# Residual by channel and projections with stationary weights in a two-layer decoder trunk on one core

## The chip, the core and the metric

One core of a Trainium2 chip runs the whole program. The metric is the device time of one execution in microseconds (us). The engines are TensorE (PE; the loads of its stationary operand are listed as PEld), VectorE (DVE), ScalarE (ACT), GpSimd (POOL) and SyncE (SP, which issues nearly all transfers). L258 is line 258 of the kernel.

## What is computed

256 tokens of width 1024 go through two layers, each with a feed-forward block before and after its mixer; four feed-forward blocks in all (l0a, l0b, l1a, l1b). Inner width is 2816.

```
def _rmsnorm(x, w):
    y = xf * lax.rsqrt(jnp.mean(xf * xf, axis=-1, keepdims=True) + NORM_EPS)
    return (y * w.astype(jnp.float32)).astype(x.dtype)
def _swiglu(h, w_in, w_out):
    gate, up = jnp.split(h @ w_in, 2, axis=-1)
    return (jax.nn.silu(gate) * up) @ w_out
for l in range(DEPTH):
    x = x + 0.5 * _swiglu(_rmsnorm(x, ffn_norm1[l]), ffn1_w_in[l], ffn1_w_out[l])
    h = _rmsnorm(x, mix_norm[l])
    if l % 2 == 0:
        x = x + _hybrid_ab_mixer(h, ...)
    else:
        x = x + _pool_mixer(h, pool_w[i], pool_scale[i])
    x = x + 0.5 * _swiglu(_rmsnorm(x, ffn_norm2[l]), ffn2_w_in[l], ffn2_w_out[l])
return _rmsnorm(x, final_norm)
```

The first mixer joins four gated DeltaNet heads (their inputs pass a short causal convolution) and four spatial-gating groups; the second averages over windows of 2 to 16 tokens.

## The kernel before, in words

**Products in three parts.** Every projection is made to nearly full fp32 accuracy from operands split into a high and a low part: hi is the value cast to fp32r (L213 or L216, ScalarE), lo is the value less hi (L214 or L217, VectorE). A product is then hi x hi + hi x lo + lo x hi, three matmuls that add up in one PSUM bank (`products`, L252 to L258). Transposes, norms and the DeltaNet algebra are plain fp32; an fp32 matmul leaves two records in the trace.

**Weights.** `load_unit` (L178) fetches one unit, mostly 1 MB, into one of four raw buffers and splits it into one of three pairs of hi and lo, 512 columns an instruction. The gain of the RMSNorm, one number per input channel, is multiplied in there (L216, L217 with a scale from `prm`).

**Residual by token.** `x` lies with tokens on the partitions. Before each block, `next_input` (L350) transposes it with TensorE (L249, 16 blocks of 128x128), splits the result into `xth` and `xtl` (channels on the partitions), and `rstd` (L235) makes the norm's factor r of each token, which scales the projections' results later.

**Feed-forward block** (`ffn`, L280). For five chunks of 512 inner columns and one of 256, gate and up are projected for each half t of 128 tokens: the token block is stationary, 512 weight columns move. ScalarE makes silu(r x gate) (L304), VectorE r x up x silu (L312). The hidden values now have tokens on the partitions, so `hidden` (L287) transposes them (L292, 44 blocks a feed-forward) and splits them into `hh` and `hl`. `out_proj` (L320) multiplies them with the output weights, hidden block stationary, 512 columns moving (L325), and VectorE adds half of it to `x` (L345). The last two units are held, so that token half 0 ends early and is prepared under the products of half 1.

**Mixer** (L459). Its projections of ba, z, sv and su work as above; q, k and v pass a convolution along the tokens and are made with the weights stationary and all 256 tokens moving (`conv`, L565, products at L577 to L579), scaled by r along the free axis (`rb`, L561, L562). Its out projection (L805) uses `out_proj`. The pool stage (`pooled`, L410) multiplies a band matrix (L425, L427) and then the pool weights.

The instruction order on each engine is fixed when the program is built: a scheduler places each instruction by its own estimates, so neighbouring steps interleave, but each engine then works through its list in order.

Of the kernel before, what the change touches and what calls it, by code (L numbers as in the profile page):

```python
# [26 lines left out]
WIDE = 130 * LINE  # L27
NEG = -1e30
# [3 lines left out]
FFN_CHUNKS = [(c * 512, 512) for c in range(5)] + [(2560, 256)]  # L32

MIX_CHUNKS = (("ba", 260), ("sv", 512), ("k", 512), ("v", 512), ("q", 512), ("z", 260), ("su", 512))

# [14 lines left out]
def weight_units():  # L50
# [3 lines left out]
    def ffn(name):  # L54
        for c, (_, w) in enumerate(FFN_CHUNKS):
            for part in ("g", "u"):
                halves = 1 if w == 256 else 2
                for h in range(halves):
                    units.append((name, "in", c, part, h, (KD // halves) * w))
        for u in range(NF // 2):  # L60
            units.append((name, "out", u, "", 0, 2 * D))

    ffn("l0a")
    for n, w in MIX_CHUNKS:
        halves = 2 if w == 512 else 1
        for h in range(halves):
            units.append(("mix", "in", n, "", h, KD // halves * w))
    for u in range(4):
        units.append(("mix", "out", u, "", 0, 2 * D))
    ffn("l0b")  # L70
    ffn("l1a")
    units.append(("pool", "w", 0, "", 0, 8 * 256))
# [8 lines left out]
def pack_weights(a):  # L81
# [4 lines left out]
    for name, kind, c, part, h, n in weight_units():  # L86
        if name in ffns:
            base, l = ffns[name]
            if kind == "in":
                c0, w = FFN_CHUNKS[c]  # L90
                c0 += DFF if part == "u" else 0
                rows = n // w * P
                src = a[base + "_w_in"][l][h * rows:(h + 1) * rows, c0:c0 + w]
            else:
                src = a[base + "_w_out"][l][c * 2 * P:(c + 1) * 2 * P]
        elif name == "mix" and kind == "in":
            rows = n // len(cols[c]) * P
            src = a["ab_w_in"][0][h * rows:(h + 1) * rows][:, cols[c]]
        elif name == "mix":
            ks = OUT_ORDER[2 * c:2 * c + 2]  # L100
            src = np.concatenate([a["ab_w_out"][0][k * P:(k + 1) * P] for k in ks])
        else:
            src = a["pool_w"][0].reshape(D, 256)
        k = src.shape[0] // P
        blocks.append(np.ascontiguousarray(src.reshape(k, P, -1).transpose(1, 0, 2)).reshape(-1))
    return np.concatenate(blocks)
# [49 lines left out]
def trunk(ctx: ExitStack, tc: tile.TileContext, x_in, xt_in, wts, prm_in, ident_in, mixc_in, band_in,  # L156
# [13 lines left out]

# [3 lines left out]
    units = weight_units()  # L174
    offsets = np.concatenate([[0], np.cumsum([u[-1] * P for u in units])])
    state = {"u": 0}

    def load_unit(k, col=None, prescale=None):  # L178
# [658 lines left out]
```

## Time and profile before

| | us |
|---|---|
| median of 3 runs (lowest, highest) | 932.19 (931.95, 934.86) |
| the profiled execution | 931.89 |
| its span, first to last instruction | 930.1 |
| PE busy in the span | 916.9 |
| DVE busy | 562.2 |
| ACT busy | 504.1 |

The mean granted TensorE clock was 0.995 of full speed. An engine's busy time is the union of its instructions' times; neighbouring matmuls overlap in the pipeline, so their mean durations don't add up to it, and the distance between starts tells what one costs in a row of many.

### The profile page before, as it was taken

How to read it: one execution, taken by the hardware profiler on the slowest of the kernel's cores; microseconds unless marked ns; L12 is line 12 of the kernel's file. 1: busy time of each engine (PE TensorE's matmuls, PEld its weight loads, DVE VectorE, ACT ScalarE, POOL GpSimd, SP SyncE). 2: the span in 40 equal slices, each digit the busy share in tenths (PEclk: the TensorE clock that was granted, in tenths of full speed). 3: DMA queues.
4: the chain of work that ended last, by engine and by line, in shares of the span. 5: the costliest groups of instructions: out<-in, count | busy, mean ns of one | idle time of the engine just before them, and what ended most of it. 6: DMA issues, size and time to landing. Idle time of an engine off the chain costs nothing.

```text
span 930.1 us, 12029 instructions
## 1 busy us (share of the span) xinstructions
PE 916.9 (99%) x4614; PEld 763.8 (82%) x4614; DVE 562.2 (60%) x987; ACT 504.1 (54%) x930; POOL 29.9 (3%) x44
## 2 busy tenths in 40 slices
PE   8999999999999999999999999999999999999997
PEld 6788888889998788888888888888888888889885
DVE  4765564468997665555644565556556565556444
ACT  6755553387747565555533565556335455556332
POOL 0000000000321000000000000000000000000000
PEclk9999999999999999999999999999999899999999
DMA  8865555534225246555455555555553365554521
GB/s 326 317 226 181 181 181 182 187 137 176 91 92 181 87 142 224 181 181 181 175 188 181 211 198 181 181 181 181 181 184 134 113 228 182 183 181 177 187 85 45
DMA packets 24521, 163.10 MB, mean 175 GB/s; under 512 B 2832, under 2 KB 2960, under 8 KB 5648
## 3 DMA queue, kind: packets, MB, share of 16 engines
q1 hardware_dynamic: 24176, 161.81, 48.9%
q8 instruction: 36, 0.59, 0.3%
q10 hardware_dynamic: 288, 0.52, 0.2%
q14 instruction: 21, 0.17, 0.1%
HBM read 161.28 MB, written 1.05 MB: 175 GB/s over the span
## 4 chain that ended last, share of the span: by engine, by line
PE 90%; DVE 4%; DMA 2%; ACT 2%; issue 1%; POOL 0%; SPq 0%; POOLq 0%; ACTq 0%
PE acc L325 26%; PE mm L258 18%; PE mm L255 18%; PE mm L256 18%; PE acc L292 2%; PE mm L325 2%; DMA x<-in_x 1%; DVE y L586 1%; PE mm L579 1%; PE acc L249 1%; DVE lo L217 1%; PE mm L577 1%; PE mm L578 1%; DMA raw<-in_wts 1%; PE acc L425 1%
## 5 line engine op out<-in xcount | busy, mean ns | idle before, releaser
L216 ACT ACTIVATE hi<-raw,prm 128x512 fp32r<-128x512 f32 (+2 forms) x448 | 268.9, 673 | 169.2 <-PE mm L258 133.7
L217 DVE SCALAR_TENSOR_TENSOR lo<-raw,prm,hi 128x512 fp32r<-128x512 f32 (+2 forms) x448 | 287.5, 699 | 120.9 <-ACT hi L216 120.7
L255 PE MATMUL mm<-hi,xth 128*128 128x512 f32 (+2 forms) x832 | 305.4, 376 | 1.5 <-ACT xth L213 1.5
L256 PE MATMUL mm<-lo,xth 128*128 128x512 f32 (+2 forms) x832 | 303.3, 373 | 0.1
L258 PE MATMUL mm<-hi,xtl 128*128 128x512 f32 (+2 forms) x832 | 207.4, 372 | 0.1
L214 DVE TENSOR_TENSOR lo<-raw,hi 128x512 fp32r<-128x512 f32 x192 | 121.3, 686 | 111.1 <-ACT hi L213 111.1
L255 PEld LDWEIGHTS mm<-hi,xth 128*128 128x128 f32 x832 | 156.5, 188 | 31.2 <-ACT xth L213 2.3
L256 PEld LDWEIGHTS mm<-lo,xth 128*128 128x128 f32 x832 | 156.6, 188 | 28.9 <-DVE lo L217 0.5
L213 ACT CAST hi<-raw 128x512 fp32r<-128x512 f32 x192 | 106.5, 619 | 131.1 <-PE acc L325 108.6
L258 PEld LDWEIGHTS mm<-hi,xtl 128*128 128x128 f32 x832 | 146.1, 188 | 29.7 <-DVE xtl L214 0.9
L325 PE MATMUL acc<-hi,hh 128*128 128x512 f32 x352 | 140.1, 398 | 0.0
L325 PE MATMUL acc<-hi,hl 128*128 128x512 f32 x352 | 138.7, 394 | 0.0
L325 PE MATMUL acc<-lo,hh 128*128 128x512 f32 x352 | 138.4, 393 | 0.0
L325 PEld LDWEIGHTS acc<-hi,hh 128*128 128x128 f32 x352 | 66.1, 188 | 15.9 <-DVE hl L214 1.2
L325 PEld LDWEIGHTS acc<-hi,hl 128*128 128x128 f32 x352 | 66.0, 188 | 15.7
L325 PEld LDWEIGHTS acc<-lo,hh 128*128 128x128 f32 x352 | 66.2, 188 | 14.4
L304 ACT ACTIVATE sg<-mm,r 128x512 f32<-128x512 f32 (+1 forms) x48 | 31.3, 653 | 54.8 <-PE mm L258 51.6
L214 DVE TENSOR_TENSOR hl<-acc,hh 128x512 fp32r<-128x512 f32 (+1 forms) x48 | 29.1, 640 | 49.5 <-ACT hh L213 49.5
L312 DVE SCALAR_TENSOR_TENSOR hid<-mm,r,sg 128x512 f32<-128x512 f32 (+1 forms) x48 | 33.7, 703 | 30.7 <-PE mm L258 30.7
L233 POOL TENSOR_TENSOR r<-ms,mhalf 128x1 f32<-128x1 f32 x14 | 8.6, 613 | 790.9 <-DVE ms L242 790.9
L239 ACT ACTIVATE junk<-x 128x512 bf16<-128x512 f32 x28 | 17.6, 629 | 24.1 <-DVE x L345 20.2
L579 PE MATMUL mm<-xth,lo 128*128 128x256 f32 x96 | 27.4, 286 | 0.0
(177 smaller groups left out, 601.7 us busy)
## 6 DMA issues: line engine op xcount, KB each, us to landing
raw<-in_wts SPq DMA_DIRECT2D x145, 1024.0 KB, 4.8
raw<-in_wts SPq DMA_DIRECT2D x2, 1040.0 KB, 5.7
raw<-in_wts SPq DMA_DIRECT2D x3, 512.0 KB, 8.2
xt<-in_xt SPq DMA_DIRECT2D x4, 256.0 KB, 7.9
x<-in_x SPq DMA_DIRECT2D x1, 1024.0 KB, 11.0
mixc<-in_mixc SPq DMA_DIRECT2D x1, 640.0 KB, 12.4
band<-in_band SPq DMA_DIRECT2D x1, 544.0 KB, 3.6
raw<-in_wts SPq DMA_DIRECT2D x2, 256.0 KB, 3.6
```

The lines of the kernel that those rows point to most:

```text
L213: act.copy(out=hi, in_=src)
L214: dve.tensor_tensor(out=lo, in0=src, in1=hi.bitcast(F32), op=ALU.subtract)
L216: act.activation(out=hi, in_=src, func=AF.Identity, scale=gain)
L217: dve.scalar_tensor_tensor(out=lo, in0=src, scalar=gain, in1=hi.bitcast(F32), op0=ALU.mult, op1=ALU.subtract)
L255: pe.matmul(out=b, lhsT=ah, rhs=wh, start=start and i == 0, stop=False)
L256: pe.matmul(out=b, lhsT=ah, rhs=wl, start=False, stop=False)
L258: pe.matmul(out=b, lhsT=al, rhs=wh, start=False, stop=stop and i == n - 1)
L292: pe.transpose(out=b[:, i * P:(i + 1) * P], in_=hid[t][:, i * P:(i + 1) * P], identity=ident)
L304: act.activation(out=s[:, :w], in_=gate[t][:, :w], func=AF.Silu, scale=r[t])
L312: dve.scalar_tensor_tensor(out=h[:, :w], in0=up[t][:, :w], scalar=r[t], in1=sg[t][:, :w], op0=ALU.mult, op1=ALU.mult)
L325: pe.matmul(out=acc[t][n], lhsT=a, rhs=w[part][:, n * 512:(n + 1) * 512], start=first and i == 0, stop=last and i == 2)
L579: pe.matmul(out=o, lhsT=wl[:, c], rhs=xth[:, k], start=False, stop=k == KD - 1)
```

## The change

- **The residual is kept by channel** (`xt`, channels on the partitions, in fp32) up to l1a. What a block adds is computed by channel too, so no transposes stand between l0a, mixer, l0b and l1a, and the separate load of x by token (1 MB) goes. Under l1a's projection 16 transposes bring the residual to tokens (`by_token`), since the pool stage and l1b's output stay by token.
- **Projections of the feed-forward blocks** go by pairs: unit f holds the 128 gate and the 128 up columns of inner block f for all eight channel blocks. Each 128x128 weight block is stationary, 256 tokens move (`products_t`). The result has the inner width on the partitions, so the hidden values need no transposes. In l1b the first 512 inner columns keep the old form.
- **Output products** of l0a, l0b and of the mixer have the weights stationary too and end channel block by channel block; those of l1a and l1b keep the old form.
- **The norm weight** is multiplied into x when it is split (`channel_done`), not into the weights; in l1b by a product with a row of it (`gb`) ahead of the transposes. The weights are split without a scale, in pieces of 1024 columns (704 in the new output units).
- **The norm factor**: squares per channel block (ScalarE), added up (VectorE), summed over channels by products with ones (`means`), then spread over the partitions (`spread`, `rb`). It scales the gate product before the silu, and the block's output at its end.
- Buffers: three raw instead of four, four pairs of hi and lo instead of three; weights are fetched two units ahead.
- The mixer's gating half of the out projection now starts before the head outputs are transposed.

The core of the diff:

```diff
+    def products_t(b, w, act_parts, start, stop, **more):
+        (wh, wl), (ah, al) = w, act_parts
+        pe.matmul(out=b, lhsT=wh, rhs=ah, start=start, stop=False, **more)
+        pe.matmul(out=b, lhsT=wh, rhs=al, start=False, stop=False, **more)
+        pe.matmul(out=b, lhsT=wl, rhs=ah, start=False, stop=stop, **more)
...
+        half = n // 2
+        for c in (slice(0, half), slice(half, n)):
+            split(hi[:, c], lo[:, c], raw[:, c])
...
+        def add(self, k):
+            act.activation(out=sq, in_=xt[:, k].rearrange("p t c -> p (t c)"), func=AF.Square)
...
+                dve.tensor_tensor(out=self.sum, in0=self.sum, in1=sq, op=ALU.add)
...
+    def channel_done(norm, k, gains):
+        src, (h, l) = xt[:, k].rearrange("p t c -> p (t c)"), x_all(k)
+        split(h, l, src, prm[:, gains + k:gains + k + 1])
+        norm.add(k)
...
-            for c, (c0, w) in enumerate(FFN_CHUNKS):
-                gate = project(w, load, c == 0, bool(early))
...
-                if waiting:
-                    hidden(*waiting)
-                up = project(w, load, False)
...
+            for f in range(f0, NF):
+                if f == 0:
+                    gate, up = bank()[:, :T], bank()[:, :T]
+                    for ks in (range(KD - 1), (KD - 1,)):
+                        for o, part in ((gate, 0), (up, KD)):
+                            for k in ks:
+                                products_t(o, ws[part + k], x_all(k), k == 0, k == KD - 1)
+                    norm.means()
+                else:
...
+                for g, gate, up in todo:
+                    dve.tensor_tensor(out=sg, in0=gate, in1=norm.rb, op=ALU.mult)
+                    act.activation(out=sg, in_=sg, func=AF.Silu)
+                    dve.tensor_tensor(out=hid, in0=up, in1=sg, op=ALU.mult)
+                    split(all_tokens(hh, g), all_tokens(hl, g), hid)
+            if name in BY_CHANNEL:
+                for d in range(KD):
+                    acc = chain(d % 2)[:, :T]
...
+                            products_t(acc, w, (all_tokens(hh, f), all_tokens(hl, f)), f == 0, f == NF - 1)
+                    dve.scalar_tensor_tensor(out=y, in0=acc, scalar=0.5, in1=norm.rb, op0=ALU.mult, op1=ALU.mult)
+                    dve.tensor_tensor(out=xs, in0=xs, in1=y, op=ALU.add)
+                    after(d)
...
+                dve.tensor_tensor(out=xg, in0=x[:, t, c], in1=gb[:, c], op=ALU.mult)
```

**How the order moves.** On PE in the feed-forward projections, before, at the end of l0a's first chunk (`xth`, `xtl` are the tokens, `hi`, `lo` the weights; `hid` the hidden values):

```order
L255 MATMUL mm<-hi,xth 128x512
L256 MATMUL mm<-lo,xth 128x512
L255 MATMUL mm<-hi,xth 128x512
L256 MATMUL mm<-lo,xth 128x512
L258 MATMUL mm<-hi,xtl 128x512 x4
L292 MATMUL acc_362<-ident,hid 128x128 x4
L292 MATMUL acc_369<-ident,hid 128x128 x4
L255 MATMUL mm<-hi,xth 128x512
L256 MATMUL mm<-lo,xth 128x512
```

and now, where its second pair ends (numbers tell tiles apart: `mm_235` and `mm_312` are the pairs' banks):

```order
L286 MATMUL mm_235<-xth_62,hi_152 128x256
L287 MATMUL mm_235<-xtl_63,hi_152 128x256
L288 MATMUL mm_235<-xth_62,lo_153 128x256
L341 MATMUL acc1_286<-rd_284,ones_68 128x256
L286 MATMUL mm_312<-xth_62,hi_161 128x256
L287 MATMUL mm_312<-xtl_63,hi_161 128x256
L288 MATMUL mm_312<-xth_62,lo_162 128x256
```

The transposes between the products are gone; triples of 256 columns follow each other, with one product against ones for the factor.

On PE at the mixer's out projection, before, around the transposes of the second half's head outputs `o` (L325 are its output products):

```order
L249 MATMUL acc_2872<-ident,o 128x128
L325 MATMUL mm<-lo,xth 128x512
L784 MATMUL acc_2853<-yv,dl_2561 128x128 x4
L249 MATMUL acc_2872<-ident,o 128x128 x3
L325 MATMUL mm<-hi,xtl 128x512
L325 MATMUL mm<-hi,xth 128x512
L325 MATMUL mm<-lo,xth 128x512
```

and now (`sgh`, `sgl` the gating half, `dnh`, `dnl` the heads'):

```order
L286 MATMUL mm<-sgh,hi 128x256
L287 MATMUL mm<-sgl,hi 128x256
L288 MATMUL mm<-sgh,lo 128x256
L271 MATMUL acc_3656<-ident,o 128x128 x4
L271 MATMUL acc_3663<-ident,o 128x128 x4
L286 MATMUL mm<-dnh,hi 128x256 x4
L287 MATMUL mm<-dnl,hi 128x256
L288 MATMUL mm<-dnh,lo 128x256
```

The transposes of both halves of `o` stand behind all gating products and ahead of all head products, where they stood among them.

On DVE in the projections, before, after l0a's first hidden blocks:

```order
L217 SCALAR_TENSOR_TENSOR lo<-raw,prm,hi 128x512 x9
L312 SCALAR_TENSOR_TENSOR hid<-mm,r,sg 128x512 x2
L217 SCALAR_TENSOR_TENSOR lo<-raw,prm,hi 128x512 x8
L214 TENSOR_TENSOR hl<-acc_532,hh 128x4x128
L214 TENSOR_TENSOR hl<-acc_539,hh 128x4x128
```

and now, in one pair:

```order
L405 TENSOR_TENSOR sg<-mm,rb 128x256
L214 TENSOR_TENSOR lo<-raw,hi 128x1024
L408 TENSOR_TENSOR hid<-mm,sg 128x256
L214 TENSOR_TENSOR lo<-raw,hi 128x1024
L214 TENSOR_TENSOR hl<-hid,hh 128x256
```

A pair has its own hidden values to make between the subtractions of its successors' weights, which are twice as long.

## Rows read from the trace of the kernel before

**Rows 1.** The page: busy time of each engine; then the last chain by engine.
```profile
PE 916.9 (99%) x4614; PEld 763.8 (82%) x4614; DVE 562.2 (60%) x987; ACT 504.1 (54%) x930; POOL 29.9 (3%) x44
PE 90%; DVE 4%; DMA 2%; ACT 2%; issue 1%; POOL 0%; SPq 0%; POOLq 0%; ACTq 0%
```

**Rows 2.** The same chain by engine, tile and line, in tenths of a per cent.
```profile
by line: PE acc L325 25.6%; PE mm L258 17.9%; PE mm L255 17.8%; PE mm L256 17.8%; PE acc L292 2.1%; PE mm L325 1.9%; DMA x<-in_x 1.2%; DVE y L586 1.0%; PE mm L579 0.9%; PE acc L249 0.9%; DVE lo L217 0.9%; PE mm L577 0.8%; PE mm L578 0.8%; i
```

**Rows 3.** Windows: stretch, length, busy per engine (count), PEclk, DMA share, GB/s.
```profile
336.00:464.00 128.00, 128.00 (x626) 106.43 (x625) 77.37 (x124) 72.53 (x126) 1.00 (x1) 1.00 0.52 184
220.00:232.00 12.00, 12.00 (x108) 12.00 (x107) 10.73 (x26) 7.05 (x14) 0.00 (x0) 1.00 0.26 91
```

**Rows 4.** Timeline, PE, l0a's projection: start us, us, instruction, count.
```profile
105.15 1.08 PE L258 MATMUL mm<-hi,xtl 128*128 128x512 f32 x4
110.71 1.10 PE L258 MATMUL mm<-hi,xtl 128*128 128x512 f32 x4
```

**Rows 5.** Chain in order of time, its longest pieces: start us, us, what.
```profile
136.89 55.35 PE acc L325 x238
463.70 55.33 PE acc L325 x238
```

**Rows 6.** Timeline, PE, the last chunk of l0a's projection.
```profile
123.62 0.28 PE L255 MATMUL mm<-hi,xth 128*128 128x256 f32 x1
126.40 0.28 PE L255 MATMUL mm<-hi,xth 128*128 128x256 f32 x1
```

**Rows 7.** Timeline, PE, inputs of the mixer's first convolution.
```profile
219.89 0.28 PE L577 MATMUL mm<-xth,hi 128*128 128x256 f32 x1
231.79 0.28 PE L577 MATMUL mm<-xth,hi 128*128 128x256 f32 x1
```

**Rows 8.** Timeline, PE, l0b: first product and first output product.
```profile
335.16 0.48 PE L255 MATMUL mm<-hi,xth 128*128 128x512 f32 x1
462.66 0.47 PE L325 MATMUL acc<-hi,hh 128*128 128x512 f32 x1
```

**Rows 9.** Timeline, PE, two fp32 kinds; each fp32 product leaves two records.
```profile
238.70 1.84 PE L601 MATMUL acc<-ones,wide 128*128 128x1 f32 x16
297.76 1.89 PE L729 MATMUL acc<-wide,sgw 128*128 128x256 f32 x8
```

**Rows 10.** Timeline, PE, transposes of the residual at l0b's end.
```profile
525.40 0.60 PE L249 MATMUL acc<-ident,x 128*128 128x128 f32 x4
525.75 0.48 PE L255 MATMUL mm<-hi,xth 128*128 128x512 f32 x1
```

**Rows 11.** Timeline, ACT, casts of the first weights, with waits.
```profile
9.06 1.33 ACT L216 ACTIVATE hi<-raw,prm 128x512 fp32r<-128x512 f32 x2 [2.40 <-DMA raw<-in_wts]
11.77 0.73 ACT L216 ACTIVATE hi<-raw,prm 128x512 fp32r<-128x512 f32 x1 [0.86 <-DMA raw<-in_wts]
```

**Rows 12.** Groups by form: busy us, mean ns of one, idle before and releaser.
```profile
L214 DVE TENSOR_TENSOR hl<-acc,hh 128x256 fp32r<-128x256 f32 x8 | 3.3, 417 | 0.0
L216 ACT ACTIVATE hi<-raw,prm 128x256 fp32r<-128x256 f32 x72 | 29.8, 503 | 9.8 <-PE mm L258 6.4 <-issue 3.5
L198 DVE TENSOR_TENSOR raw<-raw,psc 128x2048 f32<-128x2048 f32 x1 | 2.3, 2287 | 0.0
L588 ACT ACTIVATE y<-y 128x1024 f32<-128x1024 f32 x3 | 3.2, 1061 | 0.4 <-DVE y L586 0.4
L577 PEld LDWEIGHTS mm<-xth,hi 128*128 128x128 f32 x96 | 18.1, 188 | 0.0
```

**Rows 13.** Waits of PE in total, then timeline around the head outputs.
```profile
PE acc L249 <- DVE o L798: 1.9, 2, 1.0
311.85 1.05 PE L784 MATMUL acc<-yv,dl 128*128 128x128 f32 x8
317.94 0.50 PE L249 MATMUL acc<-ident,o 128*128 128x128 f32 x2 [1.01 <-DVE o L798]
```

**Rows 14.** Windows, columns as in rows 3: the pool stage.
```profile
732.00:736.00 4.00, 4.00 (x16) 3.54 (x16) 0.69 (x1) 0.58 (x1) 0.00 (x0) 0.52 0.30 125
```

More of the change, by code (lines that the diff above doesn't have):

```diff
@@ L27 @@
 WIDE = 130 * LINE
+RAW_BUFS, SPLIT_BUFS = 3, 4
 NEG = -1e30
@@ L30 @@
 LEVELS = (1, 2, 4, 8, 16, 32, 64)
-FFN_CHUNKS = [(c * 512, 512) for c in range(5)] + [(2560, 256)]
 MIX_CHUNKS = (("ba", 260), ("sv", 512), ("k", 512), ("v", 512), ("q", 512), ("z", 260), ("su", 512))
+BY_CHANNEL = ("l0a", "l0b")
+FIRST_BY_TOKEN = ("l1b",)
 def mix_columns():
@@ L54, in ffn @@
     def ffn(name):
-        for c, (_, w) in enumerate(FFN_CHUNKS):
+        f0 = 0
+        if name in FIRST_BY_TOKEN:
+            f0 = 4
             for part in ("g", "u"):
[L57 to L61, printed above, removed]
+                for h in range(2):
+                    units.append((name, "chunk", h, part, 4 * 512))
+        for f in range(f0, NF):
+            units.append((name, "pair", f, "", 2 * KD * P))
+        if name in BY_CHANNEL:
+            for d in range(KD):
+                for h in range(2):
+                    units.append((name, "outt", d, h, NF // 2 * P))
+        else:
+            for u in range(NF // 2):
+                units.append((name, "out", u, "", 2 * D))
     ffn("l0a")
@@ L229, in trunk @@
[L229 to L245 removed]
+    units = weight_units()
@@ new lines, in take, with blocks_of @@
+    def take(name, kind, ahead=2):
+        u = taken[0]
+        assert units[u][:2] == (name, kind), (units[u], name, kind)
+        taken[0] += 1
+        while len(loaded) < min(u + 1 + ahead, len(units)):
+            if units[len(loaded)][0] == "pool" and "prescale" not in special:
+                break
+            load_next()
+        return loaded[u]
+    def blocks_of(parts, w, k0, n):
+        hi, lo = parts
+        return [(hi[:, i * w:(i + 1) * w], lo[:, i * w:(i + 1) * w]) for i in range(k0, k0 + n)]
@@ L322, in some, with out_by_token @@
+    def out_by_token(name, tile_of, nu, scales, after, held=2):
+        acc = [[chain(t) for _ in range(2)] for t in range(2)]
         def some(k, w, t, n, first, last):
@@ L333, in out_proj @@
                     for n in range(2):
-                        some(ks[2 * u + i], ws[i], t, n, u == 0 and i == 0, False)
-        ws = [load_unit(2) for u in range(nu - held, nu)]
+                        some(2 * u + i, ws[i], t, n, u == 0 and i == 0, False)
+        ws = [blocks_of(take(name, "out"), D, 0, 2) for u in range(nu - held, nu)]
         for t in range(2):
@@ L454, in final @@
             queue.dma_start(out=out[t * P:(t + 1) * P, c], in_=o[:, c])
-    ffn("l1b", rr, final)
+    ffn("l1b", last, final)
 def mixer(tc, e):
@@ L568, in conv @@
             pool.memset(pre[:, :, 0:3], 0.0)
-            halves = [load(4)(0), load(4)(1)]
+            halves = load(512)
             for j in range(2):
```

454 lines of the change are left out of this document (266 added, 188 removed).

## The prediction

> **What bounds the kernel now.** I read the profile from the whole to the parts: the busy shares and the chain of waits, the chain by line, stretches of the stages, single instructions. TensorE is busy for 99% of the span, and 90% of the chain that ended last runs on it [rows 1]. By line nearly all of that is the three products of a projection (L255, L256, L258) and the output products (L325); the transposes of the hidden values (L292) hold 2.1%, and those of the residual and of the mixer's outputs (L249) 0.9% [rows 2]. Over a whole feed-forward projection TensorE is busy for all of 128.00 us, VectorE for 77.37 and ScalarE for 72.53 [rows 3]. So a term counts if it changes what TensorE has to run or makes it wait; the other engines' work counts only where it comes to stand in front of a product.
>
> A busy share doesn't price a matmul, since neighbours overlap in the pipeline. I take the pitch, from start to start over many of one kind:
> - 512 moving columns, tokens stationary: from 105.15 to 110.71 us lie 24 products, 0.2317 us each [rows 4]; in the output stage 238 run in 55.35 us, 0.2326 each [rows 5].
> - 256 columns, tokens stationary (the last chunk): 24 from 123.62 to 126.40, 0.1158 each [rows 6].
> - 256 columns, weights stationary, both token halves moving, the shape that the change uses everywhere: the mixer's convolution inputs have it already. From 219.89 to 231.79 lie 105 products, 0.1133 each [rows 7].
>
> So two products of 256 take 0.2266 us where one of 512 takes 0.2317: the new shape is not dearer, though it loads a stationary operand twice as often.
>
> **The change, part by part.** Columns are conserved. A feed-forward projection has 480 products of 512 columns and 96 of 256 now, and 1056 of 256 then.
>
> *Feed-forward in, l0b.* Before: from the first product at 335.16 to the first output product at 462.66, 127.5 us [rows 8]. Products: 480 x 0.2317 + 96 x 0.1158 = 122.3; the other 5.2 are the 44 transposes of the hidden values (L292's 2.1% of the span is 19.5 us, 4.9 in each of four [rows 2]). After: 1056 x 0.1133 = 119.6 and no transposes. Added are the norm's four one-column products (eight of the kind take 1.84 us, so 0.9) and one 256-column fp32 product against ones (four take 1.89, so 0.47) [rows 9]: 121.0. Gain 6.5.
>
> *Feed-forward in, l1a.* The same, less the transposes that bring the residual back to tokens: 16 in four groups; four start at 525.40 and the next product at 525.75 [rows 10], with a slower restart some 0.44 a group, 1.8. Gain 4.7.
>
> *Feed-forward in, l1b.* The first chunk stays by token: 96 x 0.2317 = 22.2, with eight transposes 0.9. Then 18 x 48 x 0.1133 = 97.9, and the ones product 0.5: 121.5. Gain 6.0.
>
> *Feed-forward in, l0a.* The gain of 6.5 less a later start. ScalarE's waits for weight pieces end at 9.06 and 11.77 us [rows 11], with 1.25 and 2.0 MB issued up to those pieces, so 0.277 MB per us. The long run of output products starts at 136.89, in l0b at 463.70 [rows 5]; l0b's projection began 128.5 before its run, so l0a's starts, as if dense, at 8.35. In the new order the first pair needs all of x and its own weights, 2.0 MB or 11.8 us, and the second pair 3.0 MB, 15.4 us; with 1.0 for the first half's cast it begins at 16.4, as if dense from 16.4 - 5.4 = 11.0. That is 2.6 later. The bounds are 0 (the queue goes faster once fed) and 5 (the squares that stand in front of those casts on ScalarE delay them); I take 2.6, as it goes by the rate of the same pieces. Gain 3.9.
>
> *Output products, l0a and l0b.* Now 264 x 0.2326 = 61.4 and 16 residual transposes 1.8; from 462.66 to 525.75 pass 63.1 [rows 8, 10]. Then 528 x 0.1133 = 59.8. Gain 3.4 each, 6.8. The per-channel finish (scale and add on VectorE, split, square) runs under the next channel's 66 products, 7.5 us.
>
> *Hand-overs.* After the last channel VectorE scales and adds and ScalarE casts, by 256-column rows 0.42 + 0.42 + 0.50 [rows 12], near 1.6 us with the signals. Into l0b and l1a 42 products, 4.8 us, stand before the first that needs it: nothing. Into the mixer it is 22 of 260 columns, 2.6 us; a weight subtraction of 1.2 in front of each VectorE step would break that cover. Between 0 and 1.5; I take 0.5, as the cover exceeds the bare chain.
>
> *Mixer.* Out: 96 x 0.2326 + 1.8 = 24.1 becomes 192 x 0.1133 = 21.8. The norm's products cost 1.4 and replace two of some 0.2. TensorE waited twice, 1.9 us together, for the head outputs o; from the last attention products at 311.85 to the transposes of o at 317.94 pass 6.1 us [rows 13]. The new order puts 75 side-gate products, 8.5 us, there, so both waits go; afterwards both halves of o must be cast before any product, about 1.3. VectorE is nearly full in this stage (10.73 of 12.00 us between 220 and 232 [rows 3]) and its weight subtractions, in longer pieces, get cheaper by some 9 us over the mixer, worth 0 to 3; I take 1, because TensorE is busy there too. Gain 2.3 - 1.0 - 0.5 + 0.6 + 1.0 = 2.4.
>
> *Pool.* The band is scaled instead of x, about even. But the norm weight is multiplied onto x ahead of the transposes, 0.68 for 512 columns by the slope of rows 12, twice per half of the tokens, with few products left to fill: minus 1.5 (0 to 3). TensorE's granted clock was 0.52 from 732 to 736 us [rows 14], mostly the 1.2 GHz level, after a run of small fp32 products; they remain, so I leave that in.
>
> *Covered at nothing.* Per pair of 48 products, 5.44 us, VectorE has two 1024-column subtractions and three 256-column operations. A two-operand operation takes 0.417 us for 256 columns and 2.287 for 2048 [rows 12], so 1.22 for 1024; together 3.7. ScalarE: 2 x 1.06 + 2 x 0.50 = 3.1. Both fit, and a unit is split two units, 11 us, before its use. If that cover were gone, each pair would stretch by what VectorE lacks. A pair's 1 MB in 5.44 us asks 193 GB/s against 184 now [rows 3].
>
> **Sum.** 6.5 + 4.7 + 6.0 + 3.9 + 6.8 + 2.4 - 1.5 = 28.8 us. The profiled execution took 931.89 us, 1.8 more than its span; it becomes 903.1. The median of the runs is 0.3 higher than that execution, so I say **903 us**.
>
> **A rule that speaks against it.** The rows give 0.2317 us for 512 columns and 0.1133 for 256 [rows 4, 7]. The Trainium skill, page "TensorE: Matmul & The Clock Gate", section "Back-to-back issue gap", puts the isolated gap at columns / 2.4 GHz plus a fixed 2.5 ns: by it two of 256 cost 2.5 ns more than one of 512. By that rule the change would lose 6.6 us on its 2640 halved products, where the rows give a gain near 13. The measurement decides.
>
> **Rivals.**
> 1. *The new shape runs at the other 256-column pitch.* The convolution's 0.1133 was seen with DMA at a share of 0.26; the feed-forward stage has 0.52, and its last chunk shows 0.1158 [rows 3, 6]. For it: that load. Against: there the moving operands alternate between large weight tiles, which the new shape doesn't do. Price 5280 x 0.0025 = 13.2: 916 us.
> 2. *Slower: the stationary loads come onto the path.* 5280 loads replace 2640, and one lasts 188 ns in the trace [rows 12], longer than the pitch; it is hidden only because loads overlap products. If the loads fall behind in streams ten times longer than the convolution's, every product pays. It decides from 28.8 / 5280 = 0.0055 us more, a pitch of 0.1188; at 0.125 the kernel takes 903 + 62 = 965, and with each load by itself, 0.188, 1297. Against: 105 products in a row show no drift. The Trainium skill, same page, section "The mechanism", says that a load overlaps products in flight only if it targets other rows of the array, by which every full-array load would be exposed. The convolution's rows speak against that too.
> 3. *Start and hand-overs cost more.* Start 5, mixer hand-over 1.5, pool 3, no relief of VectorE: 5.9 more, 909 us.
> 4. *Better than summed.* No clock dip in the pool stage (about 3 us) and the full relief of VectorE: 898 us.
> 5. *It doesn't do what it says.* The printed order shows 1440 and 352 triples of 256 columns and eight hidden transposes in place of 176, so hardly: 932 us.
>
> **Chances.** My forecast within its own bounds (897 to 911, rivals 3 and 4 among them) 0.78; rival 1 0.13; rival 2 0.05; VectorE as the bound in the pairs, 925 to 945, 0.02; rival 5 0.02. A measurement of this kernel can tell about 0.3%, 2.8 us. Faster 0.92, same 0.03, slower 0.05. The range goes down to 894 for the two good cases together with a start that costs nothing, and up to 918 to take in rival 1.
>
> **What would show it.** Right: hidden transposes gone but for eight; a pitch of 0.113 to 0.114 inside the pairs, 5.4 to 5.5 us a pair; l0b's first output product 121 us after its first product; no wait of more than 1.5 us outside the start; a granted clock of 1.00 but for the pool. Wrong: a pitch above 0.1188, TensorE waiting for subtracted weight halves inside the pairs, or a start that is dense only beyond 20 us.

## The result, and the profile after

The changed kernel takes **916.82 us** (median of 4 runs, 916.16 to 918.10) where the kernel before took 932.75 in the same comparison: a ratio of 0.9827, 95% interval 0.9807 to 0.9848. The forecast was 903, range 894 to 918. So the sign and the range held, and the size was off: the profiled execution's span fell by 15.4 us (930.1 to 914.7), where the steps added up to 28.8. That the range held is partly luck: its upper end, 918, was put there for rival 1, and the cause that rival 1 names is not what happened.

The page of the changed kernel: busy time per engine, then the last chain by engine.

```profile
PE 897.9 (98%) x6900; PEld 855.1 (93%) x6900; DVE 573.6 (63%) x907; ACT 456.9 (50%) x717; POOL 28.9 (3%) x40
PE 94%; DVE 3%; ACT 1%; DMA 1%; issue 0%; SPq 0%; POOL 0%; POOLq 0%; ACTq 0%; DVEq 0%
```

TensorE stays the bound, with fewer microseconds to be busy [rows 1]. A busy share can't say where the missing 13.4 us are; the starts of the stages can. An output product is one that multiplies hidden values with output weights; a pair is the 48 products that make one block of hidden values. The timeline of TensorE in the kernel before, in order: the first output product of l0a, the mixer's first product, the first output products of l1a and l1b (l0b's is in [rows 8]):

```profile
135.85 0.47 PE L325 MATMUL acc<-hi,hh 128*128 128x512 f32 x1
198.95 0.36 PE L255 MATMUL mm<-hi,xth 128*128 128x260 f32 x1
653.29 0.47 PE L325 MATMUL acc<-hi,hh 128*128 128x512 f32 x1
861.52 0.48 PE L325 MATMUL acc<-hi,hh 128*128 128x512 f32 x1
```

The same five starts in the changed kernel, and l1a's first product:

```profile
133.10 0.28 PE L286 MATMUL acc<-hh,hi 128*128 128x256 f32 x1
195.92 0.28 PE L278 MATMUL mm<-hi,xth 128*128 128x260 f32 x1
456.48 0.28 PE L286 MATMUL acc<-hh,hi 128*128 128x256 f32 x1
519.33 0.28 PE L286 MATMUL mm<-xth,hi 128*128 128x256 f32 x1
642.68 0.39 PE L437 MATMUL acc<-hi,hh 128*128 128x512 f32 x1
846.38 0.39 PE L437 MATMUL acc<-hi,hh 128*128 128x512 f32 x1
```

The differences of neighbouring rows, before and after:

| stage | before, us | after, us | gain | forecast |
|---|---|---|---|---|
| start and l0a in | 135.85 | 133.10 | 2.8 | 3.9 |
| l0a out | 63.10 | 62.82 | 0.3 | 3.4 |
| mixer and l0b in | 263.71 | 260.56 | 3.1 | 8.9 |
| l0b out and l1a in | 190.63 | 186.20 | 4.4 | 8.1 |
| l1a out, pool, l1b in | 208.23 | 203.70 | 4.5 | 4.5 |
| l1b out to the end | 68.58 | 68.32 | 0.3 | 0 |

l0b's output stage is 456.48 to 519.33, 62.85 us, against 63.1 in the forecast's own reading of the kernel before. So both output stages, with 6.8 forecast, gave 0.5. Windows of the changed kernel (stretch, length, busy of PE, PEld, DVE, ACT and POOL with counts, granted clock, DMA share, GB/s), first the pairs of l0b, then its outputs, the mixer's first convolution, and the start:

```profile
360.00:440.00 80.00, 80.00 (x708) 80.00 (x707) 51.06 (x74) 39.43 (x59) 0.00 (x0) 1.00 0.54 184
460.00:516.00 56.00, 56.00 (x472) 56.00 (x472) 35.25 (x55) 27.08 (x43) 0.00 (x0) 1.00 0.61 205
220.00:232.00 12.00, 12.00 (x108) 12.00 (x107) 10.68 (x19) 7.34 (x12) 0.00 (x0) 1.00 0.29 92
10.00:14.00 4.00, 3.64 (x17) 3.45 (x18) 3.79 (x9) 2.77 (x7) 0.00 (x0) 0.57 1.03 416
```

A count takes in two or three products that began ahead of the edge, so 80 us over 706 is **0.1133** in the pairs, the pitch that the convolution had shown [rows 7], and 56 over 470 is **0.119** in the outputs: the two stages side by side, the same shape, the clock 1.00 in both, VectorE busy for two thirds of the time and ScalarE for half. Within the output stage the spacing is between 112 and 125 ns from product to product. In l0b it follows a sequence that comes again within 1 ns with every second output block, and the 47 products beside which VectorE, ScalarE, GpSimd and the transfers all stand still have the same spacing (mean 0.1185). So contention with the other engines doesn't explain it. It had to be found in what the products read and write.

### The profile page after: what moved, and what is told of

It reads as the page before. It is cut to its first block, busy times and chain, and to the rows that moved or that the text cites. A ratio compares the mean times of both kernels' runs of the same rounds, so it can differ in the third digit from the quotient of the medians.

```text
span 914.7 us, 16344 instructions
## 1 busy us (share of the span) xinstructions
PE 897.9 (98%) x6900; PEld 855.1 (93%) x6900; DVE 573.6 (63%) x907; ACT 456.9 (50%) x717; POOL 28.9 (3%) x40
## 4 chain that ended last, share of the span: by engine, by line
PE 94%; DVE 3%; ACT 1%; DMA 1%; issue 0%; SPq 0%; POOL 0%; POOLq 0%; ACTq 0%; DVEq 0%
PE mm L286 18%; PE mm L288 18%; PE mm L287 18%; PE acc L437 13%; PE acc L288 5%; PE acc L286 5%; PE acc L287 5%; PE mm L278 2%; PE mm L279 2%; PE mm L281 2%; DMA xt<-in_xt 1%; PE acc L556 1%; PE acc L799 0%; PE acc L793 0%; PE acc L271 0%
## 5 line engine op out<-in xcount | busy, mean ns | idle before, releaser
L213 ACT CAST hi<-raw 128x1024 fp32r<-128x1024 f32 (+2 forms) x318 | 307.0, 986 | 331.7 <-PE mm L287 204.0
L214 DVE TENSOR_TENSOR lo<-raw,hi 128x1024 fp32r<-128x1024 f32 (+2 forms) x318 | 360.7, 1151 | 125.9 <-ACT hi L213 125.4
L286 PE MATMUL mm<-xth,hi 128*128 128x256 f32 x1440 | 400.9, 279 | 0.5 <-ACT xth L216 0.5
L287 PE MATMUL mm<-xtl,hi 128*128 128x256 f32 x1440 | 399.9, 278 | 0.5 <-DVE xtl L217 0.4
L288 PE MATMUL mm<-xth,lo 128*128 128x256 f32 x1440 | 399.1, 277 | 0.8 <-DVE lo L214 0.8
L286 PEld LDWEIGHTS mm<-xth,hi 128*128 128x128 f32 x1440 | 271.0, 188 | 1.5 <-ACT xth L216 0.9
L287 PEld LDWEIGHTS mm<-xtl,hi 128*128 128x128 f32 x1440 | 271.3, 188 | 1.0 <-DVE xtl L217 0.9
L288 PEld LDWEIGHTS mm<-xth,lo 128*128 128x128 f32 x1440 | 271.0, 188 | 1.2 <-DVE lo L214 1.2
L286 PE MATMUL acc<-hh,hi 128*128 128x256 f32 x352 | 99.3, 282 | 0.0
L288 PE MATMUL acc<-hh,lo 128*128 128x256 f32 x352 | 99.2, 282 | 0.0
```

The costliest lines, as they stand in the source:

```text
L213: act.copy(out=hi, in_=src)
L214: dve.tensor_tensor(out=lo, in0=src, in1=hi.bitcast(F32), op=ALU.subtract)
L286: pe.matmul(out=b, lhsT=wh, rhs=ah, start=start, stop=False, **more)
L287: pe.matmul(out=b, lhsT=wh, rhs=al, start=False, stop=False, **more)
L288: pe.matmul(out=b, lhsT=wl, rhs=ah, start=False, stop=stop, **more)
```

## Experiments

The theories at the start: A, the addresses in SBUF (the memory that the operands lie in) of what a product reads; B, the half of the bank of PSUM (the memory that products add up in) that it writes (the pairs write both, the outputs the first alone); C, a state that stays from the last interruption. All kernels are edits of the changed kernel; of each edit the lines that matter are shown, some of them shortened, with words in brackets where code is left out. e1 to e9 were executed once each, and stretches of lower clock alone move such a time by some us (e4, e8 and the pool stage show it), so the reading goes by windows and spacings.

Places in SBUF are given in KB (1000 bytes) from the start of a partition, as the sizes of the tiles add up in the order in which the kernel reserves them; they are good to about 6 KB.

**e1_fixed**

```diff
-products_t(acc, w, (all_tokens(hh, f), all_tokens(hl, f)), f == 0, f == NF - 1)
+products_t(acc, w, (all_tokens(hh, 0), all_tokens(hl, 0)), f == 0, f == NF - 1)
```

> Leaves out: the outputs of l0a and l0b multiply every weight block with the hidden state of the first 128 channels only, so they compute something else; the same 1056 products stand in the same order with the same weights. Theory A (the pitch of a product follows from which addresses of SBUF its moving tile and the weight block being loaded meanwhile have; in the changed kernel the output products run at 0.119 us in a pattern that repeats word for word every second output block): with one moving tile the pattern changes, and each half unit settles at one steady pitch, 0.1133, 0.1178 or 0.120. If 0.1133, the two output stages are 3.0 us shorter each and the kernel takes 911. Theory B (the pitch follows from the PSUM half that is written): stays at 0.119, 917. Theory C (the pitch is a state carried over from the last interruption): stays at one slow pitch, 0.1178 to 0.120, 917.

Measured: 917.36 us, and the output products at 0.119, repeating with every second output block as before. One window of l0b's outputs, e1_fixed, then e3_joined and e6_wide16 (below):

```profile
465.00:510.00 45.00, 45.00 (x381) 45.00 (x380) 27.41 (x46) 21.65 (x36) 0.00 (x0) 1.00 0.62 201
465.00:510.00 45.00, 45.00 (x381) 45.00 (x380) 27.54 (x46) 21.77 (x36) 0.00 (x0) 1.00 0.61 202
465.00:510.00 45.00, 45.00 (x381) 45.00 (x380) 27.14 (x39) 20.67 (x28) 0.00 (x0) 1.00 0.53 187
```

Which of the 22 blocks is read makes no difference. That speaks against A in the form in which I had put it (an interplay of single addresses).

**e2_halves**

```diff
-acc = chain(d % 2)[:, :T]
+if d % 2 == 0:
+    both = chain(d // 2 % 2)
+acc = both[:, d % 2 * T:(d % 2 + 1) * T]
```

> Two output blocks of l0a and l0b share one PSUM bank, the even one in its first half, the odd one in its second, as gate and up do in the pairs. Theory A (addresses of moving tile and weights in SBUF): no change, 0.119 in the same pattern, 917. Theory B (PSUM half): 0.1133 in both halves or in the second, 911 to 914. Theory C (state): 917.

Measured: 919.60. The spacing is the same in both halves, 0.119. New are longer spacings at four hand-overs in each stage, three times 0.20 and 0.22 us one behind the other and once 0.80 and 0.22; they make the two stages 2.8 us longer, which is the difference in time. B falls.

**e3_joined**

```diff
-hh = fp.tile([P, NF, 2, P], F32R, name="hh")
-hl = fp.tile([P, NF, 2, P], F32R, name="hl")
+hb = fp.tile([P, NF, 2, 2, P], F32R, name="hb")
+hh, hl = hb[:, :, 0], hb[:, :, 1]
```

> The two parts of the hidden state lie in one tile, the second part of a channel block directly behind the first (1 KB on) instead of 22 KB on. Theory A (SBUF addresses): the pattern of the pitch in the output stages changes, and its mean may fall towards 0.1133 (911) or move to 0.1178 to 0.120 (915 to 918). Theories B and C: the pattern stays as it was, 917.

Measured: 915.97, the output stages 62.70 and 62.74 us as before. The distance between the two parts doesn't matter either.

**e4_tick**

```diff
 for d in range(KD):
+    pe.matmul(out=tick[:, :1], lhsT=ident, rhs=ones[:, 0:1], start=True, stop=True)
     acc = chain(d % 2)[:, :T]
```

> One plain fp32 product of one column into a spare bank stands ahead of each of the 8 output blocks of l0a and l0b; 16 in all, about 0.2 us each with its hand-over, so 3 us if nothing else moves. Theory C (the fast or slow pitch is a state that an interruption sets anew, as after the squares' products of the norm, where pairs ran at 0.1133): the output products behind a tick run at 0.1133, 6 us less, so 914. Theories A and B: they stay at 0.119, and the kernel takes 918 to 920.

Measured: 924.36. Behind the ticks the outputs stay at 0.119; C falls for them. Each output stage is 1.6 us longer, as the ticks' price said. The rest is another matter, of the clock: between 18 and 26 us TensorE's granted clock was 0.57 here (mostly its 1.2 GHz level), and 1.00 in the changed kernel, and l0a's outputs began 3.0 us later; between 328 and 334 us it was 0.72 for 1.00, and the mixer with l0b's input took 1.7 us more.

```profile
18.00:26.00 8.00, 8.00 (x43) 8.00 (x43) 5.75 (x7) 3.81 (x4) 0.71 (x1) 0.57 0.62 203
```

**e5_xmove**

```diff
-products_t(acc, w, (all_tokens(hh, f), all_tokens(hl, f)), f == 0, f == NF - 1)
+products_t(acc, w, x_all(KD - 1), f == 0, f == NF - 1)
```

> Leaves out: the outputs of l0a and l0b multiply their weights with the last channel block of x instead of the hidden state, so they compute something else; 1056 products as before, with the moving tile where the fast pairs have theirs. Fixing the moving tile at one block of the hidden state and laying its two parts together left the pattern of 112 to 125 ns and the mean of 0.119 us untouched. Theory A2 (it is the region of SBUF in which the moving tile lies that makes the product slow: hidden state high, x low): 0.1133, the two output stages 3.0 us shorter each, 911. Theory D (it is the weight blocks, how their units are cut, or the place in the instruction stream, not the moving tile): same pattern, 0.119, 917.

Measured: 911.37. Windows of its two output stages:

```profile
140.00:190.00 50.00, 50.00 (x444) 50.00 (x443) 33.29 (x54) 25.22 (x41) 0.00 (x0) 1.00 0.64 215
460.00:516.00 56.00, 56.00 (x496) 56.00 (x496) 38.09 (x59) 29.04 (x45) 0.00 (x0) 1.00 0.64 216
```

496 products in 56 us where the changed kernel has 472: 0.1133, by another moving tile alone. Each stage takes 59.8 us, as forecast. This settles that the moving tile is what makes the outputs slow, and leaves two readings: where it lies, or what it holds.

**e6_wide16**

```diff
-units.append((name, "outt", d, h, NF // 2 * P))        (16 units)
+units.append((name, "outt", u, "", 16 * P))            (11 units)
```

> The output weights of l0a and l0b come in 11 units of 16 blocks (2048 columns, as the pairs have) instead of 16 units of 11 (1408 columns). Theory D1 (the cut of the weight units decides the pitch): 0.1133 and 911. Theory A2 (region of the moving tile) and theory D2 (place in the instruction stream): 0.119 stays on average, in another pattern at most; 916 to 917.5, since fewer and larger splits take a little off the other engines only.

Measured: 916.67, outputs at 0.119. The cut of the units doesn't change the mean. It does change the sequence: with units of 11 blocks it came again after 132 products, with units of 16 blocks it comes again after 192 (spacings within 1 ns of each other for 91% of l0b's products, against 34% at 132). Both are four units, as many as there are buffers of split weights. So where the pitch is slow, the single spacing goes with the buffer that the stationary block lies in.

**e9_probe**

```diff
+where = ("h", "a", "b", "c", "d", "e", "x", "a")[d]
+moving = (all_tokens(hh, 0), all_tokens(hl, 0)) if where == "h" else x_all(KD - 1) if where == "x" else [both parts of probes[where]]
-products_t(acc, w, (all_tokens(hh, f), all_tokens(hl, f)), f == 0, f == NF - 1)
+products_t(acc, w, moving, f == 0, f == NF - 1)
```

> Leaves out: in the outputs of l0a and l0b each of the eight output blocks multiplies its weights with one fixed small tile instead of the hidden state, so they compute something else (and one buffer less for the transfers of weights). The tile differs from block to block: 0 the hidden state itself (140 to 150 KB into a partition), 1 and 7 a copy of the first hidden block at 33 KB, 2 a copy at 62 KB (between the transferred and the split weights), 3 at 98 KB (between the two split parts), 4 at 133 KB (behind them), 5 a copy of the last block of x at 190 to 199 KB, 6 that block of x where it is (24 to 33 KB). Moving that last block of x instead of the hidden state gave 0.1133 throughout. Theory A2 (address of the moving tile): 0.1133 in blocks 1, 6 and 7, 0.119 in 0 and 5, and a boundary somewhere between 2, 3 and 4. Theory E (what the tile holds): 0.1133 in 5 and 6 alone, 0.119 in 0 to 4 and 7.

Measured: 917.28. The timeline of TensorE, the first product of each output block of l0a and the first product behind them; 66 products lie between two rows:

```profile
135.99 0.28 PE L298 MATMUL acc<-hh,hi 128*128 128x256 f32 x1
143.81 0.29 PE L298 MATMUL acc<-probea,hi 128*128 128x256 f32 x1
151.31 0.28 PE L298 MATMUL acc<-probeb,hi 128*128 128x256 f32 x1
159.14 0.28 PE L298 MATMUL acc<-probec,hi 128*128 128x256 f32 x1
167.01 0.28 PE L298 MATMUL acc<-probed,hi 128*128 128x256 f32 x1
174.85 0.28 PE L298 MATMUL acc<-probee,hi 128*128 128x256 f32 x1
182.72 0.28 PE L298 MATMUL acc<-xth,hi 128*128 128x256 f32 x1
190.27 0.28 PE L298 MATMUL acc<-probea,hi 128*128 128x256 f32 x1
197.75 0.28 PE L290 MATMUL mm<-hi,xth 128*128 128x260 f32 x1
```

| moving tile | place in the partition, about | us for 66 | pitch |
|---|---|---|---|
| hidden state | 140 to 150 KB | 7.82 | 0.1185 |
| copy of it, a | 33 KB | 7.50, 7.48 | 0.1136, 0.1133 |
| copy of it, b | 62 KB | 7.83 | 0.1186 |
| copy of it, c | 98 KB | 7.87 | 0.1192 |
| copy of it, d | 133 KB | 7.84 | 0.1188 |
| copy of x's last block, e | 199 KB | 7.87 | 0.1192 |
| x's last block itself | 24 to 33 KB | 7.55 | 0.1144 (0.1133 once settled) |

The same values are fast at 33 KB and slow at 62 and above; x's are fast where x lies and slow at 199. l0b's eight output blocks repeat it: 0.1133 to 0.1144 for a, a and x, 0.1189 to 0.1192 for the others. So it is the place, not the content, with a boundary between 37 and 62 KB while the split weights lie at about 64 to 135 KB.

**e10_far**

```diff
+far = ctx.enter_context(tc.tile_pool(name="far", bufs=1, side="right"))
-raw, hi, lo = base.tile(...)
+raw, hi, lo = far.tile(...)
```

> The whole kernel, with the transferred and the split weights at the far end of SBUF (138 to 229 KB into a partition) instead of behind x (44 to 135 KB); the hidden state moves to 49 to 104 KB, the mixer's tiles down by as much. Theory A2 with a boundary above the hidden state's new place: the output products of l0a and l0b run at 0.1133 (6.0 us less in all), the mixer's output at 0.1133 (1.0), so 910. Theory A2 with a boundary inside it: the products of the lower channel blocks at 0.1133, those above at 0.119, 911 to 916. Theory A3 (not the moving tile's address but its order to the weights': fast where it lies below them): 910 too, and the two are told apart by the blocks of the other run. Theory E (content): 917.

Measured: 937.92 (7 runs, 936.23 to 942.49), 1.0057 times the kernel before (1.0036 to 1.0077). All readings had it faster, or at worst no slower; it gives back more than the whole change won. Windows of the pairs of l0b and of its outputs:

```profile
360.00:440.00 80.00, 80.00 (x680) 80.00 (x679) 49.83 (x74) 39.08 (x60) 0.00 (x0) 1.00 0.53 185
490.00:530.00 40.00, 40.00 (x338) 40.00 (x338) 26.05 (x41) 20.07 (x32) 0.00 (x0) 1.00 0.62 208
```

The pairs, with x at its old place, have 680 products in 80 us, 0.118, where they had 708. Of what these products read only the split weights had moved, to 163 to 229 KB; the transferred weights moved too, but the 194 products beside which no transfer ran have the same spacing (0.1178). So the place of the **stationary** block counts as well, and the fast pitch needs both; A2 was half of the rule. A3 falls: x lies below the weights here, and its products are slow.

**e7_mixorder**

```diff
 for u in range(2):
     for i in range(2):
         for d in range(KD):
             some(OUT_ORDER[2 * u + i], i, w, d)
+        if (u, i) in ((0, 0), (0, 1)):
+            out_tiles(dn_parts, oa[i], i, ...)
-for t in range(2):
-    out_tiles(dn_parts, oa[t], t, ...)
```

> In the mixer's output the transposes of o stand between the groups of 24 products of the first half instead of behind all 96. Theory M1 (the changed mixer loses time because the transposes of o, ready at 316.4, stand in TensorE's queue behind products until 319.5, and the first product of dnh then waits 1.3 us for its split): the wait of dnh (1.3) and of dnl (0.7) go, about 2 us less, 915. Theory M2 (the mixer is bound by its serial chain on VectorE and ScalarE, and the products only fill it): the wait moves to the transposes, 917.

Measured: 916.47. In the changed kernel, TensorE around the head outputs:

```profile
319.46 1.04 PE L271 MATMUL acc<-ident,o 128*128 128x128 f32 x8
321.80 0.39 PE L286 MATMUL mm<-dnh,hi 128*128 128x256 f32 x1 [1.30 <-ACT dnh L216]
340.67 0.95 PE L327 MATMUL acc<-ones,sq 128*128 128x1 f32 x8
```

In e7_mixorder:

```profile
315.85 0.30 PE L271 MATMUL acc<-ident,o 128*128 128x128 f32 x1 [1.31 <-DVE o L929]
339.15 0.95 PE L327 MATMUL acc<-ones,sq 128*128 128x1 f32 x8
641.14 0.39 PE L437 MATMUL acc<-hi,hh 128*128 128x512 f32 x1
```

Both theories were partly right. The waits for dnh and dnl are gone, a wait of 1.31 for o itself stands in their place, since I had put the transposes too early, and 1.5 us stay won up to l1a's outputs (641.14 for 642.68). In this execution the pool stage took 1.5 us more, by its clock: 0.53 against 0.69 between 717 and 728 us, first e7_mixorder, then the changed kernel.

```profile
717.00:728.00 11.00, 11.00 (x45) 9.73 (x45) 2.77 (x4) 1.90 (x4) 0.00 (x0) 0.53 0.01 6
```

```profile
717.00:728.00 11.00, 11.00 (x52) 9.66 (x52) 2.77 (x4) 1.90 (x4) 0.00 (x0) 0.69 0.15 65
```

That this is the edit's doing isn't shown. From l1a's first output product to l1b's, kernels whose pool stage is the same take 202.2 us (e3_joined) and 202.3 (e9_probe), 203.7 (changed kernel), 205.2 (e7_mixorder) and 205.4 (e12_fused2), and the granted clock between 705 and 745 us goes with it: 0.96 in the first two, 0.91, and 0.87 in the last two. So one profile of a kernel can differ from another by 3 us here.

**e8_poolsq**

```diff
-act.activation(out=sq, in_=xs, func=AF.Square)
+pool.tensor_tensor(out=sq, in0=xs, in1=xs, op=ALU.mult)     (first norm only)
```

> The eight squares of the first norm are taken on GpSimd instead of ScalarE. Theory S1 (the start is bound by ScalarE, which takes splits of x, splits of weights and squares in turn, 0.41 us for each square, and by the slow clock that follows the holes): three or four squares lie ahead of the last split of x, so it ends 1.2 us sooner, the pairs of f from 1 on begin 1 to 1.5 us sooner, 915.5. Theory S2 (the start is bound by the transfers): nothing moves, 917.

Measured: 924.98, 8 us slower, of which 6.8 stand at l0a's first output product. The edit made a new chain:

```profile
4.85 1.19 POOL L318 TENSOR_TENSOR sq<-xt 128x256 f32<-128x256 f32 x2 [3.62 <-DMA xt<-in_xt]
12.45 0.61 POOL L318 TENSOR_TENSOR sq<-xt 128x256 f32<-128x256 f32 x1 [6.42 <-DVE sq L324]
```

There are two buffers for squares, so GpSimd's third waits 6.42 us for VectorE's first sum, and each later one for the sum before it; the norm comes late. Not all of the loss is this chain: TensorE's granted clock was 0.51 between 21 and 28 us, and e4_tick lost 3.0 us at its start with such a stretch and no such chain. The run doesn't tell S1 from S2: what bounds the start stays open.

**e11_fused** takes the outputs of l0a and l0b two hidden blocks at a time, so that the moving tile can lie near x:

```diff
+near = base.tile([P, 2, 2, 2, P], F32R, name="near")    (behind x, two hidden blocks)
-for d in range(KD):  (22 blocks into one output block, 8 times, behind all pairs)
+for g in (f - 2, f - 1):  (2 blocks into 8 output blocks, behind every second pair)
+    for d in range(KD):
+        out_product(w, g, d)
```

> The whole kernel. The outputs of l0a and l0b no longer wait for all 22 blocks of the hidden state: after every second pair the two blocks before it are multiplied into all eight output blocks at once (four PSUM banks, two blocks in each), so only two blocks of the hidden state are held, at 33 to 37 KB into a partition, behind x; the last four blocks are taken output block by output block, two of them from tiles at 137 to 150 KB. x's own float copy moves to the far end, and the mixer's low part of su takes the near tile. Theory A2 (the moving tile's address decides; 33 KB was fast, 62 KB and all above it slow): 432 of the 528 products of each stage at 0.1133 for 0.119, 2.5 us less in each, and 0.2 to 0.3 from the block pair 18 and 19; what is lost is at the ends, where eight blocks are finished within 9 us instead of 63 (VectorE about 1.7 us a block): up to 2 us each. So 911.5 to 915. Theory E2 (the order of the output stage, every product of it one block further, makes it slow, wherever the tile lies): the products stay at 0.119 and the ends cost, 917 to 920.

Measured: 922.65 (4 runs, 920.11 to 925.45). These products stood behind the evaluation of block f, so even blocks were read after block f had been written over f-2 (the output then uses other blocks), and each hand-over cost about 0.4 us (in l0b one comes every 16.73 us, where the next run needs 16.32 for the same products). Between the stops the products from the near tile came 0.1133 to 0.1142 us apart, but for two groups in l0a at 0.118; the late ones came at 0.119: A2's part of the expectation held and E2's fell, the time did not.

**e12_fused2** puts them ahead of that evaluation, and takes e7_mixorder's transposes behind 24 and 72 products:

```diff
+if name in BY_CHANNEL and f % 2 == 0 and 2 <= f < NF - 2:
+    w = blocks_of(take(name, "outt"), P, 0, 2 * KD)
+    for g in (f - 2, f - 1): ... out_product(w, g, d)
 ...
-if name in BY_CHANNEL and f % 2 == 0 and 2 <= f < NF - 2:   (the same lines, behind the evaluation)
...
+if (u, i) in ((0, 0), (1, 0)):                              (in the mixer, among its output products)
+    out_tiles(dn_parts, e["oa"][t], t, ...)
```

> The whole kernel. As in the run before it (e11_fused), the outputs of l0a and l0b are taken two blocks of the hidden state at a time, right behind every second pair, from a tile at 33 to 37 KB; but the products of blocks f-2 and f-1 now stand ahead of the evaluation of block f, which writes over the place of f-2 (there it stood behind it, so the products read the wrong block and waited about 0.9 us at each of the 18 hand-overs). The transposes of o in the mixer's output stand behind 24 and behind 72 of the 96 products of its first half. Theory A2 (address of the moving tile): 480 products of each stage at 0.1133 instead of 0.119, 2.7 us each, 5.5 in all; mixer 1.3 to 2 less; ends, where eight blocks are finished within 9 us, up to 2 us more each. Sum 909.5 to 914. Theory F (finishing eight blocks at once makes VectorE the bound at the ends, over 3 us each, and the reading and rewriting of the small tile stalls ScalarE's queue): 916 or above.

Measured: **913.14** (5 runs, 910.73 to 913.53), 0.9784 of the kernel before (0.9761 to 0.9807): ahead of the changed kernel's 0.9827 too. Window of l0b, pairs and outputs in turn:

```profile
346.00:496.00 150.00, 150.00 (x1326) 150.00 (x1326) 86.01 (x115) 69.59 (x96) 0.00 (x0) 1.00 0.55 191
```

150 us over 1324 is 0.1133, outputs included, without one wait. PE's waits from 295 to 345 us (what waits, what it waits for, us in all, times, longest) hold nothing of o or dnh any more:

```profile
PE acc L882 <- DVE wide L871: 0.5, 1, 0.5
PE mm L286 <- ACT sgh L213: 0.2, 1, 0.2
```

l1a's outputs begin 5.5 us sooner than in the changed kernel:

```profile
637.20 0.39 PE L459 MATMUL acc<-hi,hh 128*128 128x512 f32 x1
```

The pool stage took 1.7 us more in this execution (205.4 us to l1b's outputs against 203.7, a difference of the clock as in e7_mixorder), so 3.6 of the span are left. The edits of outputs and mixer were not run apart, so the run as a whole doesn't price them singly. The ends, where four blocks remain for each output block, run at 0.119 to 0.122.

## Why the prediction was right and wrong

- **Feed-forward in: right.** The pairs run at 0.1133, the forecast's own sign of being right, no product waits for a weight half in 360 to 440, and l1b with the pool gained 4.5, as forecast. l1a's 4.7 came out near 4.2: l0b out and l1a in gained 4.4, of which the outputs had 0.2. The first pair there ran at 0.118, and the four groups of by-token transposes stand in that stretch; what each has of it wasn't taken apart.
- **Rule against rows: right in the pairs alone.** Two products of 256 cost 0.2266 there, less than one of 512; in the outputs they cost 0.238, more. By the formula for the isolated gap in the Trainium skill, page "TensorE: Matmul & The Clock Gate", section "Back-to-back issue gap", one of 256 columns comes to 109 ns, an estimate. The rows show 113 or 119, so its fixed part is not one number here.
- **Output products: the term that failed.** I read 0.1133 off the convolution [rows 7] and took it for 528 products of each output stage, as the shape was the same. The convolution moves x, which lies at the start of SBUF; the outputs move the hidden state, at 141 KB and beyond, and run at 0.119: 62.8 us for 59.8. That a pitch belongs to the shape, wherever the operands lie, was the step that failed; e5_xmove and e9_probe show that this alone is the difference. It cost 6.3 of the 13.4 that are missing, and at 2 x 0.119 = 0.238 the new form is dearer than the old one's 0.2326; what the stages still won are the transposes. A warning stood in my own rows: 0.1158 beside 0.1133 [rows 6]. I took it for rival 1, a matter of load, instead of asking what else those two differ in; what makes it 0.1158 no run here tells. The forecast's own sign of being wrong, a pitch above 0.1188, was met in these two stages.
- **Rivals 1 and 2: neither; rival 3 in part.** The time of rival 1, 916, is nearly what came, by another cause: the pitch isn't one for the kernel, it is 0.1133 under a DMA share of 0.54, and in the outputs 0.119 also beside products where no transfer runs. Rival 2's price didn't come, though the outputs lie just above the break-even pitch of 0.1188 that it named; a load lasts 188 to 189 ns in the trace at either pitch, so the loads don't show what makes the outputs slow. Of rival 3 came a dearer hand-over in the mixer and no relief of VectorE.
- **Mixer: wrong by 5.8, with l0b's input.** Its 192 output products move tiles from 166 KB up and run at 0.1185: 1.0 us. The hand-over that I priced at 1.3 was 2.0 (dnh 1.3, dnl 0.7), 0.7 more: when o was ready, at 316.4, 26 products still stood in TensorE's queue ahead of its transposes, until 319.46; e12_fused2 removes the wait. VectorE's relief, taken at 1, didn't come: 10.68 of 12.00 between 220 and 232, against 10.73 [rows 3]. From the mixer's first product to the one that begins the gate (L860, at 296.61; in the kernel before 297.76 [rows 9]) pass 100.7 us for 98.8, a loss of 1.9 where the terms of that stretch (the norm's products, the hand-over, the relief) came to a loss of 0.5: 1.4. TensorE waits for inv, rd and df there. l0b's input takes 121.6 for the 121.0 forecast, from behind the last head product (335.44) and with the six of its products that stood among the head products: 0.6. The last 2.1 lie between the gate and that product and weren't taken apart.
- **Start: 2.8 for 3.9.** The estimate by the rate of the pieces was near. TensorE's granted clock was 0.57 between 10 and 14 us (1.00 from 8 to 16 in the kernel before), but that isn't shown to be the reason. e1_fixed has the same start, its clock was 1.00 there, and its l0a outputs began at 134.16, later than the changed kernel's 133.10. In the kernels with this start (e1 to e7) they begin between 132.8 and 136.1 us, so a miss of 1.1 lies within what executions with the same start differ by.
- **Pool: right in sum, in part by luck.** I left its low clock in; it was there (0.69 from 717 to 728). But other executions of the same stage took 1.5 us less or 1.7 more.

The sum of the misses: outputs 6.3, mixer with l0b's input 5.8, start 1.1, l1a 0.5, less 0.3 at the end. Two lines that this account rests on, the product that begins the gate in the changed kernel, and the window of e1_fixed's start:

```profile
296.61 1.97 PE L860 MATMUL acc<-wide,sgw 128*128 128x256 f32 x8 [0.53 <-DVE wide L849]
```

```profile
8.00:16.00 8.00, 6.20 (x43) 5.19 (x42) 5.83 (x14) 5.29 (x14) 0.00 (x0) 1.00 0.99 357
```

## What to carry to other kernels

A pitch read from one place of a trace is the pitch of that shape with those operands: before it is carried over to another stage, look whether its operands lie in the same part of SBUF. By these runs, what TensorE streams and loads most belongs near the start of SBUF, raw transfers and what only the other engines touch behind it; a hidden state that is too large for that can be used up two blocks at a time. And before a gain or loss of 1 to 3 us is put down to an edit, compare the granted clock and the length of the stages that the edit doesn't touch: here the same pool stage took 202.2 to 205.4 us.

## What was not expected of the hardware

- The pitch of a fp32r product of 256 columns depends on where both operands lie: 0.1133 with x or a copy at 16 to 37 KB and weights at about 64 to 135 KB; about 0.119 with the moving tile at 62 KB or above; 0.118 with x low and weights at 163 to 229 KB. Why it is so, and where the boundary for the weights lies between 135 and 163 KB, no run tells; a layout with the hidden state whole and low was not run, as there was no room for it beside the mixer.
- With both operands in the fast places a pair can still run at 0.118: l0b's f = 2, from 347 to 353 us, behind the product that spreads the norm, and then 0.1133 from the next pair on. In e8_poolsq three pairs behind the first norm run at 0.117 to 0.118, from 31 to 48 us. What sets it and ends it stays open.
- The mean of the slow products, 0.119, doesn't change with the block that moves (e1), the PSUM half (e2) or the distance of the two parts (e3). Their single spacings repeat with the cycle of the four weight buffers, after 132 products in units of 11 blocks and after 192 in units of 16.
